# Idle products and turns among gate products, a longer fill at a branch, a later weight split: three reorderings in a two-layer trunk kernel

## The chip, the cores and the metric

The kernel runs on one core of a Trainium2 chip. The metric is the device time of one execution in microseconds. The core's engines are named as in the profile: PE is TensorE (its matrix products; PEld its weight loads), DVE is VectorE, ACT is ScalarE, POOL is GpSimd and SP is SyncE. Each has a queue of instructions of its own, which it works through in order.

## The reference

16 learned meta tokens are put ahead of a sequence of 512 tokens with 1024 features. Two layers follow, each with an RMSNorm, a combined input projection, a mixing branch, a SiLU gate and an output projection that is added to the stream; then a final norm.

```python
def gla_branch(xn, w_in, w_gate_up, b_gate, gnorm, w_out):      # 4 heads
    proj = xn @ w_in
    q, k, v, z, g_lr = jnp.split(proj, ...)                     # g_lr has 16 columns
    lg = jax.nn.log_sigmoid((g_lr @ w_gate_up + b_gate)) / GLA_TAU
    ...                                                         # chunks of 64 with decay exp(cumsum(lg))
    y = jax.nn.silu(z) * o
    return y @ w_out

def diff_branch(xn, w_in, lam_vecs, gnorm, w_out, rel_table, lambda_init):   # 8 heads
    q, k, v, z = jnp.split(xn @ w_in, 4, axis=-1)
    ...
        p = jax.nn.softmax(s, axis=-1)                          # two score maps per head
        a = p[:, :, 0] - lam * p[:, :, 1]
        return jnp.einsum('bhqk,bhkv->bhqv', a, vh)
    ...
    y = jax.nn.silu(z) * head_rms(o) * gnorm * (1 - lambda_init)
    return y @ w_out

h = concatenate([meta, x])
for i in range(2):
    h = h + (gla_branch, diff_branch)[i](rmsnorm(h, g_norm[i]), ...)
return rmsnorm(h[16:], g_final)
```

## The kernel before, in words

**Number format.** Every factor of a product is held as two parts, a rounded one and the rest: `split` (L264 on ACT makes the first, L265 on DVE the second; names end in h and l, as in `wh`, `wl`, `a11h`, `a11l`, and `x`). A product takes three passes (h·h, h·l, l·h). The sequence of 528 is worked on in two halves of 264 columns, so most PE instructions are 128x128 weights by 264 columns.

**Products.** A `Unit` computes a projection of 256 columns with seven block products in place of eight, out of sums of token blocks (`token_sums`, L743 to L752: `X["t1"]` to `X["t4"]`) and sums of weight blocks (`want_unit`, L325). Its block products accumulate in banks named `bx`, `by` and `bv` (L386); after some of them `partial` (L407, ACT, high priority) copies the bank out as `u`, and the next block product goes on adding in the same bank, so PE waits there for `u`. `add` (L432 to L436, DVE) makes the outputs. The first head's q, k and v are plain products instead (`plain_unit`, L825).

**Weights.** `Weights` is a queue of weight loads. A load (SP, one or two transfers of 512 KB) fills a `raw` buffer, of which there are two; its parts (`a11`, `sum`, `pair` and so on) are split as soon as there is room for them.

**Order.** PE's order is the order in which the code is written. `W` (a `Weaver`) holds products that are due later, and `W.fill(us)` takes products worth so many microseconds out of that queue and puts them between two steps. ACT and DVE are also ordered by hand up to the gate products (the block `ordered`); after that a scheduler orders them by priority, and `urgent` gives a call a higher one.

**The gate stage.** After the normalised tokens are turned (`turned`, L666) and split, the gate's 16 columns are computed for all tokens: eight steps k, each of two halves in two banks (`pgs`, L939), with `W.fill(0.6)` from the fourth step on, which takes v's products (L825). The banks are then read by ACT (L946, L949) and DVE (L947, L948, L950). v's second half is accumulated in the same two banks afterwards. `wur` (L953 on ACT, L954 on DVE) is the split of the gate's second factor. `raw_turn` (L654) turns the raw tokens of blocks 0, 3 and 4 on PE, and `raw_copy` (L660 on ACT, L662 on DVE) copies them to `hT`.

**The steepness branch.** A flag `fl` (L996, L997) says whether the decays are so steep that another way of computing scores is needed. PE carries it to one partition (L1220), DVE turns it into an integer `fi` (L1221), all engines load it (L1223) and branch (L1224). With these inputs the branch is not taken.

**The second layer's scores and values.** For each block of 128 tokens: scores and softmax (L1575 to L1582), a turn of the probabilities (L1590, L1591; `aT` and `am` on ACT and DVE), values (L355, L1606), norm (`output`: L1610, L1611 and L1614 on ACT, L1613 on POOL) and `rows` (L1620 on PE, L1623 on DVE). They run between the block products of the units of the next head.

Of the kernel before, what the change touches and what calls it, by code (L numbers as in the profile page):

```python
# [20 lines left out]
P = 128  # L21
# [187 lines left out]
def trunk(ctx, tc, x, meta, g_norm, gla_w_in, gla_w_gate_up, gla_b_gate, gla_gnorm, gla_w_out,  # L209
# [30 lines left out]
    def pb_pair():  # L240
        turns[0] += 1
        return [pb_tile(tag) for tag in (("bx", "bx") if turns[0] % 2 else ("bv", "by"))]

    def ps_tile():
        return T(ps_pool, [P, 512], F32, "ps")
# [12 lines left out]
        return run  # L258


    def split(hi, lo, src, scale=None):

        if scale is None:
            act.activation(hi, src, AF.Copy)  # L264
            dve.tensor_tensor(lo, src, hi.bitcast(F32), op=ALU.subtract)  # L265
        else:
            act.activation(hi, src, AF.Copy, scale=scale)
            dve.scalar_tensor_tensor(lo, src, scale, hi.bitcast(F32), op0=ALU.mult, op1=ALU.subtract)
# [39 lines left out]

    def block_pair(src):
        wh, wl = w_pair([P, 2, 512])
        split(wh, wl, src)
        return [[t[:, i, :] for t in (wh, wl)] for i in range(2)]

    def want_unit(w, c0):
        def single(tag, b):
            def fn(raw):
                t = [T(wp, [P, 512], F32R, tag + part, bufs=1) for part in "hl"]
                split(*t, raw[:, b, :])  # L320
                return t
            return Part(tag, fn)

        def add(o, a, b):
            dve.tensor_tensor(o, a, b, op=ALU.add)  # L325
# [20 lines left out]
    def want_plain(w, c0):  # L346

        return ws.want((w, c0), [Part("pair", lambda raw: block_pair(raw[:, 0::3, :])),
                                 Part("pair", lambda raw: block_pair(raw[:, 1:3, :]))])

    def mm3(ps, a, b, first=True, last=True, **kw):
# [39 lines left out]
    class Unit:  # L391
# [12 lines left out]
        @urgent  # L404
        def partial(self):
            t = T(up[0], [P, HT], F32, "u", bufs=3)[:, :self.n]
            act.activation(t, self.bx[:, :self.n], AF.Copy, scale=self.sc)  # L407
            return t

        def first(self):  # L410
# [165 lines left out]
    dve.memset(mhalf, -0.5)  # L576
    warm = ps_tile()

    def warm_up(n):
        for _ in range(n):  # L580
            pe.matmul(warm[:, :P], ones, ones, start=True, stop=True)

    warm_up(10)

# [14 lines left out]
    glr_raw = T(gp, [P, KT, RANK], F32, "a0")  # L599
    sp.dma_start(glr_raw, g_w_in[:, 6144:6160].rearrange("(k p) c -> p k c", p=P))  # L600

    v_first = [want_plain(g_w_in, 2048 + c) for c in (0, 256)]
    ws.held = 1
    ws.fetch()
    wup = v2[1][:, 0, :]
# [43 lines left out]
    def raw_turn(b):  # L649
        n = BLK[b][1]  # L650
        raws[b] = [ps_tile().rearrange("p (k c) -> p k c", k=4) for _ in range(2)]
        for i, pt in enumerate(raws[b]):
            for k in range(4):
                pe.transpose(pt[:, k, :n], xt[b][:n, (4 * i + k) * P:(4 * i + k + 1) * P], ident[:n, :n])  # L654

# [72 lines left out]
    for k0 in range(0, KT, 2):  # L728
        if k0 + 2 < KT:
            scaled_pair(k0 + 2)  # L730
        i, ks = k0 // 4, slice(k0 % 4, k0 % 4 + 2)
        for n, o in enumerate((X[("b11", "b21")[i]], (b12, X["b22"])[i])):
            split(o[0][:, ks, :], o[1][:, ks, :], xg[i][:, ks, n * HT:(n + 1) * HT])
        if k0 in (0, 4):
            ws.make_one()
    ws.held = 0
    x1, x2 = xg[0][:, :, :HT], xg[0][:, :, HT:]
    x3, x4 = xg[1][:, :, :HT], xg[1][:, :, HT:]
# [194 lines left out]
    heads = [Head() for _ in range(G_HEADS)]  # L933
    q_gla_v(0, heads[0])
    pgs = pb_pair()
    for k in range(KT):
        for n in range(2):
            for i, x in enumerate((X["b11"], b12) if k < 4 else (X["b21"], X["b22"])):
                pe.matmul(pgs[i][:112, :HT], glr[:, k, :], x[n][:, k % 4, :],  # L939
                          start=k == 0 and n == 0, stop=k == KT - 1 and n == 1)  # L940
        if k >= 3:
            W.fill(0.6)
    gh = T(gp, [P, L], F32R, "a0")
    for i, pg in enumerate(pgs):
        cs = slice(i * HT, (i + 1) * HT)
# [10 lines left out]
    carry = T(gp, [P, L], F32, "c0")  # L956
    dve.memset(carry, 1.0)
    dve.memset(carry[:, NM::P], 0.0)
    for b in (0, 3, 4):
        raw_turn(b)  # L960
        raw_copy(b, 0, dve)
        raw_copy(b, 1, act)
# [255 lines left out]
    W.fill(2.4)  # L1218
    pf = ps_tile()
    pe.matmul(pf[0:1, 0:1], fl[:, 1:2], one1, start=True, stop=True)  # L1220
    dve.tensor_copy(fi, pf[0:1, 0:1])  # L1221
    W.fill(1.5)
    steep = nc.values_load(fi[0:1, 0:1], min_val=0, max_val=P)  # L1223
    with tc.If(steep > 0, label="steep"):  # L1224

# [244 lines left out]
    def turned_back2(s, m, vt, first=False):  # L1470
        if not first:

            urgent(dve.tensor_copy)(vt[:, HT:HT + 8], vt[:, 2 * HT:2 * HT + 8])

        @urgent
        def post():
            end = L if first else 272
            pt, pm = to_tokens(vt, RBLK if first else HBLK, vt[:, end - 32:end])
            cs = slice(m * P, (m + 1) * P)
            split3(s.vm[:, cs], pm, 32, short[:, NM + 1:NM + 2])  # L1480
            split(s.v[0][:, :, cs], s.v[1][:, :, cs], pt.rearrange("p (b c) -> p b c", b=4))

        def done(pt, one, m):
            landed(s.v[0][:, :, m * P:m * P + P], s.v[1][:, :, m * P:m * P + P], pt, one)

        def last(pm):
            split3(s.vm, pm, 32, short[:, NM + 1:NM + 2])

        if first or s is heads[-1]:
            W.defer(2.2 if first else 1.4, post)  # L1490
        else:
            if m:
                s.leave = turn_by_dma(T(ep, [P, 2, 536], F32, "planes", bufs=1),
                                      [(slice(3, 1, -1), 0), (slice(1, None, -1), 272)], 240, 3.0 if heads.index(s) % 2 else 11.0, done, last)
            s.leave(m, vt[:, :536])
# [347 lines left out]
```

## Time and profile before

| | |
|---|---|
| median of 3 runs | 990.0 us (989.08 to 992.66) |
| the profiled execution | 992.34 us |
| its span in the trace | 990.5 us |
| mean granted clock of PE | 0.994 |
| PE busy | 971.0 us, 98% |
| DVE busy | 778.7 us, 79% |
| ACT busy | 614.2 us, 62% |
| POOL busy | 53.2 us, 5% |
| transfers | 96.24 MB, mean 97 GB/s |

Times in the trace count from the start of the span. A row of the timeline gives the start, the length, the engine, the line and the operation, the tiles out and in, and how many instructions are taken together; in brackets stands the engine's idle time before it and what ended that. The instructions of a row overlap, since a PE pass lasts longer than the distance to the next. PEclk is the share of full clock that PE was granted.

### The profile page before, as it was taken

The numbers are of one execution on the slowest core, as the hardware profiler recorded it, in microseconds if no ns is written. First come the engines' busy times: TensorE is split into PE (matmuls) and PEld (weight loads), VectorE is DVE, ScalarE is ACT, GpSimd is POOL, SyncE is SP. The second block draws the span as 40 slices with busy tenths as digits, with TensorE's granted clock in tenths as the row PEclk, the third lists the DMA queues.
The fourth block names the chain that finished last, engine by engine and source line by source line (L and its number), as shares of the span: only waits on it lengthen the run. The fifth ranks groups of instructions, "written<-read, shape, count | busy, mean of one in ns | idle before, by whom it ended". The sixth has DMA issues, their size and how long they took to land. (4 is left out here: it accounts for less than half of the span.)

```text
span 990.5 us, 18146 instructions
## 1 busy us (share of the span) xinstructions
PE 971.0 (98%) x7043; PEld 915.6 (92%) x7043; DVE 778.7 (79%) x1586; ACT 614.2 (62%) x1304; POOL 53.2 (5%) x68
## 2 busy tenths in 40 slices
PE   8999999999999999999999999999999999998997
PEld 7999999999999999999999998898988989988896
DVE  7888886887778788556998885977958879676785
ACT  7675865465547656536657675576764667654583
POOL 1000000001000100000000001001110000000001
PEclk8999999999999999999999999999999999999999
DMA  8223323742373322222332624235253352631222
GB/s 194 76 52 87 89 68 111 144 109 54 108 160 86 86 66 78 72 85 86 96 86 77 154 63 137 74 97 137 83 146 85 97 135 72 159 86 54 86 65 85
DMA packets 150472, 96.24 MB, mean 97 GB/s; under 512 B 33117, under 2 KB 136829, under 8 KB 150384
## 3 DMA queue, kind: packets, MB, share of 16 engines
q1 hardware_dynamic: 147504, 89.61, 33.7%
q10 hardware_dynamic: 2880, 5.46, 1.6%
q8 instruction: 55, 0.90, 0.4%
q14 instruction: 33, 0.27, 0.1%
HBM read 83.64 MB, written 7.57 MB: 92 GB/s over the span
## 5 line engine op out<-in xcount | busy, mean ns | idle before, releaser
L265 DVE TENSOR_TENSOR wl<-raw,wh 128x1024 fp32r<-128x1024 f32 x99 | 120.7, 1220 | 26.5 <-ACT wh L264 19.6
L264 ACT ACTIVATE wh<-raw 128x1024 fp32r<-128x1024 f32 x99 | 104.1, 1053 | 53.3 <-PE by L918 27.5
L386 PE MATMUL bx<-x,wh 128*128 128x264 f32 (+1 forms) x640 | 95.6, 287 | 3.0 <-ACT u L407 2.8
L386 PE MATMUL bv<-x,wh 128*128 128x264 f32 (+1 forms) x656 | 97.2, 286 | 0.2 <-DVE t L432 0.2
L386 PEld LDWEIGHTS bx<-x,wh 128*128 128x128 f32 x640 | 84.9, 189 | 4.1 <-ACT u L407 3.3
L386 PEld LDWEIGHTS bv<-x,wh 128*128 128x128 f32 x656 | 86.3, 189 | 0.7 <-DVE t L432 0.4
L376 PE MATMUL bx<-x,wh 128*128 128x512 f32 (+1 forms) x256 | 62.5, 386 | 0.0
L265 DVE TENSOR_TENSOR wl<-sum,wh 128x1024 fp32r<-128x1024 f32 x41 | 50.1, 1221 | 14.9 <-ACT wh L264 12.9
L407 ACT ACTIVATE u<-bx 128x264 f32<-128x264 f32 (+1 forms) x120 | 45.4, 379 | 25.1 <-PE bx L386 23.2
L1613 POOL TENSOR_TENSOR st<-st,mhalf 128x1 f32<-128x1 f32 x32 | 33.0, 1032 | 467.1 <-ACT on L1611 415.5
L1577 ACT ACTIVATE p<-p,st 128x528 f32<-128x528 f32 (+3 forms) x64 | 36.4, 568 | 31.1 <-DVE st L1575 30.7
L386 PE MATMUL bv<-x,wl 128*128 128x264 f32 (+1 forms) x328 | 55.2, 285 | 0.0
L386 PE MATMUL bx<-x,wl 128*128 128x264 f32 (+1 forms) x320 | 54.0, 287 | 0.0
L376 PEld LDWEIGHTS bx<-x,wh 128*128 128x128 f32 x256 | 44.5, 188 | 8.0
L264 ACT ACTIVATE wh<-sum 128x1024 fp32r<-128x1024 f32 x41 | 43.3, 1055 | 12.1 <-PE bv L386 4.5
L264 ACT ACTIVATE a11h<-raw 128x512 fp32r<-128x512 f32 x41 | 25.8, 628 | 38.5 <-DMA raw<-in_diff_w_in_dram 22.0
L386 PE MATMUL by<-x,a12h 128*128 128x264 f32 (+1 forms) x320 | 46.7, 285 | 0.0
L386 PE MATMUL bx<-x,a11h 128*128 128x264 f32 (+1 forms) x320 | 46.2, 285 | 0.0
L386 PEld LDWEIGHTS bv<-x,wl 128*128 128x128 f32 x328 | 45.9, 188 | 0.0
L386 PEld LDWEIGHTS bx<-x,wl 128*128 128x128 f32 x320 | 45.4, 190 | 0.5 <-DVE wl L265 0.2
L386 PEld LDWEIGHTS bx<-x,a11h 128*128 128x128 f32 x320 | 42.2, 188 | 0.8
L386 PEld LDWEIGHTS by<-x,a12h 128*128 128x128 f32 x320 | 41.8, 188 | 0.1
(475 smaller groups left out, 2640.4 us busy)
## 6 DMA issues: line engine op xcount, KB each, us to landing
raw<-in_gla_w_in_dram SPq DMA_DIRECT2D x48, 512.0 KB, 4.2
raw<-in_diff_w_in_dram SPq DMA_DIRECT2D x42, 512.0 KB, 5.6
raw<-in_diff_w_in_dram SPq DMA_DIRECT2D x11, 1024.0 KB, 6.1
raw<-in_gla_w_out_dram SPq DMA_DIRECT2D x8, 1024.0 KB, 5.3
raw<-in_diff_w_out_dram SPq DMA_DIRECT2D x8, 1024.0 KB
vd<-planes ACTq DMA_DIRECT2D x12, 268.0 KB, 3.5
vd<-keep ACTq DMA_DIRECT2D x8, 264.0 KB, 2.3
T<-bdr SPq DMA_DIRECT2D x8, 264.0 KB, 3.4
```

Source lines behind the costliest of these rows:

```text
L264: act.activation(hi, src, AF.Copy)
L265: dve.tensor_tensor(lo, src, hi.bitcast(F32), op=ALU.subtract)
L376: pe.matmul(bank, a[:, k, :], b[k] if n0 is None else b[k][:, n0 + i * nn:n0 + (i + 1) * nn], start=n == 0 and ks[0] == 0, stop=n == len(t ...
L386: pe.matmul(bank[:, :x[q].shape[2]], w[p][:, k * P:(k + 1) * P], x[q][:, k, :], start=first and i == 0, stop=i == len(PASSES) - 1, skip_gr ...
L407: act.activation(t, self.bx[:, :self.n], AF.Copy, scale=self.sc)
L1577: act.activation(p[:, :nk], p[:, :nk], AF.Exp, scale=-1.0, bias=st[:, m:m + 1], accum_out=st[:, 2 + m:3 + m])
L1613: pool.tensor_tensor(ms, ms, mhalf[:, :1], op=ALU.pow)
```

## The change

It has three parts.

**In the gate stage**, eleven products of a tile of ones with itself (`warm_up`) are put among the four gate products of the first step, into a bank that nobody reads. The fills begin at the second step instead of the fourth. The turns of token blocks 3 and 4 move from behind the gate products to places among steps 1 to 4, and their copies to `hT` are all made by ACT; only block 0 is still turned afterwards. DVE's half of the first split of v's weights (`keep`) is issued one step of x splits later.

**At the branch**, the fill between the flag's product and its load grows from 1.5 to 3.2 us, and DVE's conversion of the flag gets a higher priority.

**In the last head of the second layer**, the split of the first block (`a11`) of its v unit is issued after the last partial sum that was copied out (`issue_after(W.moved.ins)`) instead of as early as it can be.

```diff
+    kept = []
+
+    def split(hi, lo, src, scale=None, keep=False):
-        if scale is None:
+        if keep:
+            act.activation(hi, src, AF.Copy)
+            kept.append(lambda: dve.tensor_tensor(lo, src, hi.bitcast(F32), op=ALU.subtract))
+        elif scale is None:
...
-    def want_unit(w, c0):
+    def want_unit(w, c0, calm=False):
         def single(tag, b):
             def fn(raw):
                 t = [T(wp, [P, 512], F32R, tag + part, bufs=1) for part in "hl"]
-                split(*t, raw[:, b, :])
+                with tc.issue_after(W.moved.ins) if calm and b == 0 else ExitStack():
+                    split(*t, raw[:, b, :])
                 return t
...
         def partial(self):
             t = T(up[0], [P, HT], F32, "u", bufs=3)[:, :self.n]
-            act.activation(t, self.bx[:, :self.n], AF.Copy, scale=self.sc)
+            W.moved = act.activation(t, self.bx[:, :self.n], AF.Copy, scale=self.sc)
             return t
...
-    v_first = [want_plain(g_w_in, 2048 + c) for c in (0, 256)]
+    v_first = [want_plain(g_w_in, 2048 + c, c == 0) for c in (0, 256)]
...
         if k0 in (0, 4):
             ws.make_one()
+        if k0 == 2:
+            kept.pop()()
...
     pgs = pb_pair()
+    idle = pb_tile("bv")
+    turns_of = {(2, 2): (3, 1), (2, 3): (4, 0), (4, 0): (4, 1)}
     for k in range(KT):
         for n in range(2):
             for i, x in enumerate((X["b11"], b12) if k < 4 else (X["b21"], X["b22"])):
+                if k == 0:
+                    warm_up((3, 3, 1, 4)[2 * n + i], idle)
+                if (k, 2 * n + i) in turns_of:
+                    b, half = turns_of[k, 2 * n + i]
+                    raw_turn(b, [half])
                 pe.matmul(pgs[i][:112, :HT], glr[:, k, :], x[n][:, k % 4, :],
                           start=k == 0 and n == 0, stop=k == KT - 1 and n == 1)
-        if k >= 3:
+        if k >= 1:
             W.fill(0.6)
+        if k == 1:
+            raw_turn(3, [0])
+        if k == 5:
+            for b in (3, 4):
+                for i in range(2):
+                    raw_copy(b, i, act)
...
-    for b in (0, 3, 4):
+    for b in (0,):
         raw_turn(b)
...
-    dve.tensor_copy(fi, pf[0:1, 0:1])
-    W.fill(1.5)
+    urgent(dve.tensor_copy)(fi, pf[0:1, 0:1])
+    W.fill(3.2)
...
-        return W.add(Unit(want_unit(d_w_in, 2 * DI + 256 * hd), X, 1.0, dst, lambda i: turned_back2(s, i, vts[i])), 9.2)
+        u = want_unit(d_w_in, 2 * DI + 256 * hd, hd == D_HEADS - 1)
+        return W.add(Unit(u, X, 1.0, dst, lambda i: turned_back2(s, i, vts[i])), 9.2)
```

The changed kernel has other line numbers: L265 becomes L270, L268 L273, L386 L392, L407 L413, L747 L757, L748 L758, L825 L835, L946 to L950 become L969 to L973, L954 becomes L977, L1220 and L1223 become L1243 and L1246, and L1610, L1614 become L1634, L1638.

DVE's queue behind the last x splits, before. The banks of the gate products are `bx_314` and `bx_315`; `y` and `x` are token sums and their splits:

```order
L265 TENSOR_TENSOR x_4_80<-y_35_258,x_4_80 128x1056
L947 CAST a_20_157<-bx_314 16x264
L948 CAST a_20_157<-bx_314 16x264
L954 TENSOR_TENSOR z_392<-v_13_120,z_392 32x1024
L950 TENSOR_TENSOR a_20_157<-bx_314,a_49_380 16x264
L947 CAST a_20_157<-bx_315 16x264
L948 CAST a_20_157<-bx_315 16x264
L662 COPY hT_90<-ps_398 128x4x16
L662 COPY hT_90<-ps_410 128x4x128
L950 TENSOR_TENSOR a_20_157<-bx_315,a_49_380 16x264
L662 COPY hT_90<-ps_422 128x4x128
L748 TENSOR_TENSOR y_42_292<-y_42_292,y_35_258 128x4x264
```

The same place in the changed kernel:

```order
L270 TENSOR_TENSOR x_4_80<-y_35_258,x_4_80 128x1056
L758 TENSOR_TENSOR y_42_291<-y_42_291,y_35_258 128x4x264
L970 CAST a_20_157<-bx_314 16x264
L971 CAST a_20_157<-bx_314 16x264
L670 COPY hT_90<-ps_446 128x4x16
L977 TENSOR_TENSOR z_440<-v_13_120,z_440 32x1024
L973 TENSOR_TENSOR a_20_157<-bx_314,a_54_428 16x264
L970 CAST a_20_157<-bx_315 16x264
L971 CAST a_20_157<-bx_315 16x264
L273 SCALAR_TENSOR_TENSOR x_5_81<-y_42_291,x_5_81 128x1056
L973 TENSOR_TENSOR a_20_157<-bx_315,a_54_428 16x264
L762 TENSOR_TENSOR y_42_291<-y_42_291 128x4x264
```

The token sum of L748 (now L758) and the split of the next one (L273) stand ahead of the last read of the second bank, and two of the copies to `hT` are gone from this queue.

PE's queue at the branch, before (`by_1078` is the bank of the next unit's first product):

```order
L825 MATMUL bx_988<-x_3_79,wh_893 128x264
L1220 MATMUL ps_1044<-ones,fl_1003 1x1
L825 MATMUL bx_987<-x_2_78,wh_893 128x264
...
L825 MATMUL bx_988<-x_3_79,wl_894 128x264
L386 MATMUL by_1078<-x_1_77,a11h_904 128x264 x3
L1223 TENSOR_LOAD fi_1007
```

The same place in the changed kernel:

```order
L835 MATMUL bx_1000<-x_3_79,wl_906 128x264
L1243 MATMUL ps_1068<-ones,fl_1027 1x1
L392 MATMUL by_1090<-x_1_77,a11h_916 128x264 x8
L392 MATMUL by_1090<-x_1_77,a11l_917 128x264 x4
L392 MATMUL bx_1113<-x_2_78,a12h_1077 128x264 x8
L392 MATMUL bx_1113<-x_2_78,a12l_1078 128x264 x4
L392 MATMUL by_1090<-x_5_81,wh_1073 128x264 x6
L1246 TENSOR_LOAD fi_1031
```

The flag's product stands behind the plain unit's last product instead of 12 ahead of it, and 30 products stand between it and the load instead of 15.

ACT's queue at the start of the last head's units, before (`raw_13837` is the last head's v weights, `raw_13710` an earlier load, `bx_13881` the bank of the running unit):

```order
L264 ACTIVATE a11h_14046<-raw_13837 128x512
L1610 ACTIVATE ps_13909<-st_13657 128x1
L1611 ACTIVATE on_13920,st_13657<-ps_13909 128x257
L1614 ACTIVATE on_13920<-ps_13909,st_13657 128x256
L264 ACTIVATE wh_13970<-raw_13710 128x1024
L407 ACTIVATE u_13937<-bx_13881 128x264
L264 ACTIVATE a12h_14117<-raw_13837 128x512
```

In the changed kernel the row of `a11h` is gone from ahead of `on`, and stands further down:

```order
L1638 ACTIVATE on_13932<-ps_13921,st_13669 128x256
L269 ACTIVATE wh_13982<-raw_13722 128x1024
L413 ACTIVATE u_13949<-bx_13893 128x264
L269 ACTIVATE a12h_14129<-raw_13849 128x512
L269 ACTIVATE aT_2534_13970<-ps_13964 128x256
L368 ACTIVATE am_13969<-ps_13965 32x128
L369 ACTIVATE am_13969<-ps_13965 32x128
L413 ACTIVATE u_13998<-bx_13893 128x264
L269 ACTIVATE a11h_14058<-raw_13849 128x512
```

Two partial sums and the norm's steps now come before the first block's split; its DVE half moves likewise, from ahead of the weight sums (L325) to behind `yt` (L1623).

More of the change, by code (lines that the diff above doesn't have):

```diff
@@ L258, in urgent @@
         return run
-    def split(hi, lo, src, scale=None):
-        if scale is None:
+    kept = []
[4 more added lines that the diff above has]
+        elif scale is None:
             act.activation(hi, src, AF.Copy)
@@ L305, in halves_of, with block_pair @@
         return [Part("pair", lambda raw, ca=ca: split_w(raw, ca)) for ca in (0, c)]
-    def block_pair(src):
+    def block_pair(src, keep=False):
         wh, wl = w_pair([P, 2, 512])
-        split(wh, wl, src)
+        split(wh, wl, src, keep=keep)
         return [[t[:, i, :] for t in (wh, wl)] for i in range(2)]
-    def want_unit(w, c0):
+    def want_unit(w, c0, calm=False):
         def single(tag, b):
@@ L344, in want_unit, with want_plain @@
         return a11, a12, a22, s21, s43
-    def want_plain(w, c0):
-        return ws.want((w, c0), [Part("pair", lambda raw: block_pair(raw[:, 0::3, :])),
+    def want_plain(w, c0, keep=False):
+        return ws.want((w, c0), [Part("pair", lambda raw: block_pair(raw[:, 0::3, :], keep)),
                                  Part("pair", lambda raw: block_pair(raw[:, 1:3, :]))])
@@ L577, in trunk, with warm_up @@
     warm = ps_tile()
-    def warm_up(n):
+    def warm_up(n, t=None):
+        t = warm if t is None else t
         for _ in range(n):
-            pe.matmul(warm[:, :P], ones, ones, start=True, stop=True)
+            pe.matmul(t[:, :P], ones, ones, start=True, stop=True)
     warm_up(10)
@@ L647, in scaled, with raw_turn @@
             dve.tensor_scalar(o, xt[b][:n, i * 512:(i + 1) * 512], sums0[:n, 5 + b:6 + b], None, op0=ALU.mult)
-    def raw_turn(b):
+    def raw_turn(b, halves=range(2)):
         n = BLK[b][1]
-        raws[b] = [ps_tile().rearrange("p (k c) -> p k c", k=4) for _ in range(2)]
-        for i, pt in enumerate(raws[b]):
+        for i in halves:
+            pt = ps_tile().rearrange("p (k c) -> p k c", k=4)
+            raws.setdefault(b, []).append(pt)
             for k in range(4):
```

## The prediction

> **What bounds the kernel now.** I read the page's busy shares first, then the list of what TensorE (PE) waited for, then windows, then the timeline around each wait.
>
> ```profile
> PE 971.0 (98%) x7043; PEld 915.6 (92%) x7043; DVE 778.7 (79%) x1586; ACT 614.2 (62%) x1304; POOL 53.2 (5%) x68
> ...
> PE bx L386 <- ACT u L407: 2.8, 1, 2.8
> PE by L386 <- PEq L1224: 1.7, 1, 1.7
> ...
> PE bx L825 <- DVE a L950: 0.5, 1, 0.5
> ```
>
> PE is busy for 98% of the span. Only time in which PE stands still, or runs at half clock, can be won. The change aims at the two longest single waits (2.8 and 1.7 us), and at the gate stage, where PE seems busy. There the windows must be read with their clock (columns: window, length, busy us and instructions of PE, PEld, DVE, ACT, POOL, then PEclk, DMA share, GB/s):
>
> ```profile
> 12.29:15.70 3.41, 3.04 (x26) 2.61 (x25) 2.61 (x6) 2.82 (x7) 0.60 (x3) 1.00 1.17 290
> 15.70:19.12 3.42, 2.46 (x10) 1.50 (x10) 3.26 (x5) 3.42 (x7) 0.22 (x1) 0.99 1.10 210
> 19.12:22.53 3.41, 2.86 (x12) 2.40 (x12) 3.41 (x6) 3.36 (x6) 0.00 (x0) 0.50 0.39 21
> 22.53:25.95 3.42, 3.42 (x17) 3.42 (x17) 3.38 (x5) 0.14 (x1) 0.00 (x0) 0.51 0.56 90
> 80.54:83.95 3.41, 1.75 (x15) 1.57 (x14) 3.41 (x7) 0.77 (x2) 0.00 (x0) 1.00 0.05 12
> 906.57:909.98 3.41, 0.63 (x5) 0.64 (x6) 3.15 (x5) 2.70 (x8) 0.55 (x1) 1.00 0.02 6
> 909.98:913.40 3.42, 3.42 (x18) 3.42 (x18) 2.94 (x8) 0.90 (x4) 0.00 (x0) 0.50 0.00 0
> 913.40:916.80 3.40, 3.40 (x28) 3.36 (x28) 1.99 (x5) 1.75 (x6) 0.99 (x1) 1.00 0.00 0
> ```
>
> The bounds are multiples of 3.41 us from 19.12, where the clock steps. A window with 10 passes (15.70) or 5 (906.57) is followed by one at 0.50; one with 15 (80.54) is not; 12 passes at half clock leave it at half, 17 bring it back. So the clock follows how much PE did in the window before. A full window at half clock does 18 passes instead of 28, and costs at most 3.41 / 2 = 1.7 us.
>
> **A, the gate stage.** Before, PE ends the gate products, the transposes and the first half of v's products, and then stands until VectorE (DVE) has freed the second accumulator bank:
>
> ```profile
> 15.74 1.36 DVE L265 TENSOR_TENSOR x<-y,x 128x528 fp32r<-128x528 f32 x2 [0.42 <-ACT x L264]
> 17.22 1.23 DVE L265 TENSOR_TENSOR wl<-raw,wh 128x1024 fp32r<-128x1024 f32 x1
> ...
> 24.53 1.25 DVE L743 TENSOR_TENSOR y<-y 128x1056 f32<-128x1056 f32 x1
> ...
> 31.24 1.22 DVE L954 TENSOR_TENSOR z<-v,z 32x1024 fp32r<-32x1024 f32 x1 [1.46 <-ACT z L953]
> 32.49 0.42 DVE L950 TENSOR_TENSOR a<-bx,a 16x264 fp32r<-16x264 f32 x1
> ...
> 35.89 1.26 DVE L748 TENSOR_TENSOR y<-y,y 128x1056 f32<-128x1056 f32 x1
> 38.38 1.25 DVE L268 SCALAR_TENSOR_TENSOR x<-y,x 128x1056 fp32r<-128x1056 f32 x1
> 17.65 1.18 ACT L264 ACTIVATE x<-y 128x528 fp32r<-128x528 f32 x2
> 28.90 0.43 DVE L947 CAST a<-bx 16x264 fp32r<-16x264 f32 x1 [0.66 <-ACT a L946]
> 12.10 0.83 PE L581 MATMUL ps<-ones 128*128 128x128 f32 x6
> 13.71 1.91 PE L666 MATMUL ps<-ident,y 128*128 128x128 f32 x16
> 29.83 1.53 PE L654 MATMUL ps<-ident,v 128*128 128x128 f32 x12
> 34.44 0.28 PE L825 MATMUL bx<-x,wh 128*128 128x264 f32 x1
> 35.19 2.09 PE L825 MATMUL bx<-x,wh 128*128 128x264 f32 x15 [0.47 <-DVE a L950]
> ```
>
> PE's side gets faster. A 264-wide product costs (2.09 - 0.28) / 15 = 0.12 us at full clock, an idle pass (0.83 - 0.27) / 5 = 0.11, a transpose (1.53 - 0.27) / 11 = 0.115. From the end of the sixteen L666 transposes (about 15.6) to the end of v's first half there are 80 products (9.6 us), 11 idle products of two passes (2.5), 16 transposes (1.8) and the eight small ones of block 0 (0.6): 14.5 us, so 30.1 if PE never waits; with some waits for x I take 30.6. Before it was 34.56. The window from 15.70 gets about 13 more passes, so the half clock from 19.12 goes.
>
> But who frees the banks? DVE is what is late next. The moved wl makes it wait for ScalarE's (ACT) second x half (done 18.83, row at 17.65): about 0.4 us lost, so L743 starts at 24.9. From there, by before's spacings, L747 26.2, x 27.3. L748, which was behind the bank at 35.89, now stands ahead of it: 28.5. Then the casts at 29.7 and 30.15 (PE's last gate product ends at about 28.6, no wait), the small hT copy 30.6, L954 30.85, the first L950 32.1, the two casts to 33.4, L268's split (ahead of the bank now, 1.17) to 34.7, the second L950 to 35.1. PE's second product of v's second half waits for that: 35.1 to 35.3 against 35.19. The hT copies that went to ACT, and DVE's 0.66 and 1.46 of idle time in these rows, pay for L748 and L268 and nothing more. Gain: 0.0. DVE comes out some 2 to 3 us ahead, which nobody needs: in the list of waits above, PE's next one is the branch's.
>
> And PE now stands from 30.6 to 35.2, but for a product or so: 4.5 us, longer than the 2.85 at 906.5 that cost a window at half clock, and than the 1.66 in the branch that cost none. Cost: nothing, if PE's side is slower than worked; 0.8 to 1.7 by most positions of the 3.41 us window; 2.25 with the windows as in this trace (32.77 to 36.18 with only 1.1 us of work in it: 0.55 lost; 36.18 to 39.59: 1.7). I take 1.7, the row at 909.98. A: -1.7 (0 to -2.3).
>
> **B, the steepness branch.**
>
> ```profile
> 78.56 0.15 DVE L997 TENSOR_SCALAR fl<-fl 128x1 f32<-128x1 f32 x1
> 79.15 0.19 PE L1220 MATMUL ps<-ones,fl 128*1 128x1 f32 x2
> ...
> 81.68 0.14 DVE L1221 CAST fi<-ps 1x1 int32<-1x1 f32 x1
> ...
> 80.83 0.53 PE L386 MATMUL by<-x,a11h 128*128 128x264 f32 x3
> 83.01 0.84 PE L386 MATMUL by<-x,a11h 128*128 128x264 f32 x5 [1.66 <-PEq L1224]
> ```
>
> fi comes 3.1 us after fl (DVE does a wl and an x split between them), and PE takes its next product 83.01 - 81.82 = 1.19 after fi. Now 30 products (3.65 us) stand between L1220 and the load of fi instead of 15, and L1220 and the last decay product each stand 12 products later. On DVE a sum and a ks add (about 1.0 together) come in ahead of the cast: fi is 3.5 after fl. If fl comes as long after the last decay product as now (6.9, for L1220's 7.3), PE resumes at 6.9 + 3.5 + 1.19 = 11.6, with its products done at 7.3 + 3.65 = 10.95: 0.6 of the wait stays. DVE arrives less loaded, so I take 0.2. The price of the fill is none: the 15 products are only done earlier. On DVE and ACT the load of fi now stands behind a11, sum, the z add and raw (2.4 us), so the kd of the first scores comes later; PE has 69 products (8 us) before it reads kd. Gain 1.5 (1.0 to 1.66).
>
> **C, the last head's first block.**
>
> ```profile
> 905.68 0.63 ACT L264 ACTIVATE a11h<-raw 128x512 fp32r<-128x512 f32 x1 [4.14 <-DMA raw<-in_diff_w_in_dram]
> 906.22 0.16 ACT L1610 ACTIVATE ps<-st 128x1 f32<-128x1 f32 x1
> ...
> 908.91 0.38 ACT L407 ACTIVATE u<-bx 128x264 f32<-128x264 f32 x1
> 907.26 0.69 DVE L325 TENSOR_TENSOR sum<-raw 128x512 f32<-128x512 f32 x1 [0.23 <-DMA raw<-in_diff_w_in_dram]
> ...
> 910.67 0.41 DVE L265 TENSOR_TENSOR aT<-ps,aT 128x256 fp32r<-128x256 f32 x1
> 902.96 0.28 PE L1606 MATMUL ps<-vm,am 96*128 96x256 f32 x1
> 909.35 1.63 PE L386 MATMUL bx<-x,wh 128*128 128x264 f32 x8 [2.85 <-ACT u L407]
> ...
> 913.76 0.88 PE L355 MATMUL ps<-v,aT 128*128 128x256 f32 x6
> 920.89 0.38 PE L355 MATMUL ps<-v,aT 128*128 128x256 f32 x1 [0.16 <-DVE aT L265]
> ```
>
> ACT sits 4.14 us on a weight block, with L1610 and the partial sum u behind it; L1610's input was there at 903.24. From L1610 to PE's product are 909.35 - 906.22 = 3.13 us, so without a11h PE goes on at 906.4, and at once, since its queue reaches that product at 906.5: 2.85 won, and the 1.7 of half clock from 909.98.
>
> What is late next is DVE's queue. Its sum waits for the same load (second half, 907.26), and aT stands five instructions behind: 910.67 + 0.41 = 911.1, unchanged. PE's third L355 needs it; with full clock PE is there at 909.6 and waits 1.5. That product began at 914.0 before: 2.9 won there, in place of 4.5. Then ACT: L1610 of the next scores follows an hT that comes out of the same DVE queue at about 913.2; 2.7 us more (906.22 to 908.91) to the end of its wh, which now stands ahead of the k splits, 1.3 for these (0.63 per 128x512, by a11h), and aT at about 917.5; DVE's part stands behind a wl (1.23) and two k splits (0.69 each) that wait for these, about 919.2. PE wants it at 917.8. The product that began at 920.89 begins at 919.2: gain 1.7. a11h itself is needed only by the unit behind. C: 1.7, from 1.6 to 2.9 (if DVE gets to aT first).
>
> **The sum.** 0.0 - 1.7 + 1.5 + 1.7 = 1.5 us gained. The profiled execution took 992.34 (span 990.5 and 1.84 around it), 2.34 above the median of the runs, 990.0. It becomes 990.8; I take the 1.5 off the median: 988.5.
>
> **The rivals.**
>
> *A pays in full.* If DVE reached the banks at PE's pace, its six operations on them (0.42 to 0.43 each) would follow the last gate product at 28.6 through ACT: 31.6 instead of 35.2, 3.6 won and no standing PE. With B and C 6.8: 983.2. For it: PE's side really is 4 us earlier. Against: the order of DVE's queue is fixed.
>
> *The bank as worked, but no clock loss*: 986.8. For it: 80.54, where 15 passes kept the clock; with PE slower by 0.5 the first window gets there.
>
> *C is empty*: DVE and the next load hold PE to the old time; 990.2. Against: the third L355 is released at 911.1 in any case.
>
> *The clock falls anyway, and A turns into a loss.* If transposes and idle products did not hold the clock, 19.12 to 25.95 would stay at half with more work in it (two more fills of six products, 16 transposes: 3.2 us at full clock). DVE's cast at 29.7 tolerates a last gate product that ends 0.8 late; every microsecond more moves both banks. Ending at 33.0 instead of 28.6, it moves them by 3.5; with the 1.7 behind it, 5.2 against 3.2 from B and C: 992.0, slower. The rows speak against it: 12.29 to 15.70 held six idle passes, no other ordinary product, and twenty L666 transposes, and the window behind it ran at 0.99, where five ordinary passes (906.57) did not do. The Trainium skill, "TensorE: Matmul & The Clock Gate", Part 4: PE-mode transpose, says that a transpose does not count as PE-busy in the same way and doesn't engage the full clock. By that rule this rival would be the likely one; this trace's 0.99 after a window of transposes disagrees, and the measurement decides.
>
> **How the numbers follow.** Half a per cent, 5 us, is about what a measurement of this kernel can tell from no change. Forecast (988.5) 0.49, no clock loss (986.8) 0.18, A in full (983.2) 0.17, C empty (990.2) 0.07, A a loss (992.0) 0.09. Faster than 985.05: A in full, and 0.01 for "no clock loss" with C at 2.9 and B at 1.66 (985.4) and PE a little quicker: 0.18. Slower than 994.95: the last rival where the last gate product ends another 3 us later, 0.04. Within: 0.78. The range leaves out the outer parts of the first and the last rival: 983.0 to 992.0.
>
> **What would show it.** A: windows from 15.70 to 25.95 at 1.00, v's first half ended by about 30.6, PE waiting some 4 us for L950's successor until 35.2, a window at 0.50 from about 36. A resume before 33 there proves me wrong. B: no wait over 0.7 at the branch. C: no wait for u; 1 to 1.6 for aT at 911, again about 1.3 at 919, clock 1.00.

## The result, and the profile after

The changed kernel takes 994.53 us (median of 20 runs, 992.92 to 995.14), the kernel before 991.04 in the runs beside it (20 runs, 988.27 to 994.83). The ratio is 1.0032, 95% interval 1.0022 to 1.0042: slower by 0.32%, inside the half per cent, but outside the predicted range, and with the wrong sign. The profiled execution took 995.14 (span 993.4), where before's took 992.34 (990.5).

PE's busy time on the page, and the longest entries of what it waited for:

```profile
PE 972.2 (98%) x7065; PEld 917.5 (92%) x7065; DVE 778.1 (78%) x1584; ACT 615.6 (62%) x1306; POOL 52.2 (5%) x68
...
PE bx L835 <- DVE a L973: 4.8, 2, 2.5
...
PE bx L392 <- DVE fi L257: 1.1, 1, 1.1
...
PE ps L992 <- DVE t L998: 0.9, 1, 0.9
PE bx L392 <- ACT u L413: 0.8, 2, 0.6
...
PE ps L361 <- DVE aT L270: 0.7, 1, 0.7
```

The two waits that the change aimed at, 2.8 for u and 1.7 in the branch, are gone. In their place stand 4.8 at the gate's banks, 1.1 in the branch and 0.7 for aT.

**The gate stage.** The windows from before's clock steps, then those on the changed kernel's own steps (of PE alone: busy, passes, clock, DMA):

```profile
12.29:15.70 3.41, 3.13 (x29) 2.94 (x28) 2.87 (x8) 2.87 (x7) 0.79 (x2) 1.00 1.16 300
15.70:19.12 3.42, 3.42 (x32) 3.42 (x31) 2.53 (x4) 3.42 (x7) 0.24 (x1) 1.00 1.05 219
19.12:22.53 3.41, 3.41 (x31) 3.41 (x30) 3.41 (x6) 3.28 (x6) 0.00 (x0) 1.00 0.47 23
...
31.25:34.66 3.41, 0.39 (x1) 1.00 0.00 0
34.66:38.07 3.41, 2.25 (x10) 0.50 0.02 5
38.07:41.49 3.42, 3.42 (x18) 0.50 0.00 0
41.49:44.90 3.41, 3.41 (x30) 1.00 0.00 0
```

And DVE's and PE's timelines:

```profile
28.89 1.25 DVE L758 TENSOR_TENSOR y<-y,y 128x1056 f32<-128x1056 f32 x1
30.17 0.43 DVE L970 CAST a<-bx 16x264 fp32r<-16x264 f32 x1
...
31.34 1.22 DVE L977 TENSOR_TENSOR z<-v,z 32x1024 fp32r<-32x1024 f32 x1
32.59 0.42 DVE L973 TENSOR_TENSOR a<-bx,a 16x264 fp32r<-16x264 f32 x1
...
33.96 1.26 DVE L273 SCALAR_TENSOR_TENSOR x<-y,x 128x1056 fp32r<-128x1056 f32 x1
35.25 0.42 DVE L973 TENSOR_TENSOR a<-bx,a 16x264 fp32r<-16x264 f32 x1
...
33.07 0.39 PE L835 MATMUL bx<-x,wh 128*128 128x264 f32 x1 [2.48 <-DVE a L973]
35.82 2.54 PE L835 MATMUL bx<-x,wh 128*128 128x264 f32 x10 [2.36 <-DVE a L973]
```

PE ran at full clock to 30.6 (33.07 - 2.48) and then stood for 4.84 us but for one product. It went on at 35.82, where before it went on at 35.19, and did so at half clock until 41.49: v's first half ends four us earlier (30.59 instead of 34.56) and wins nothing, and two windows at half clock are paid.

**The branch**, on DVE and PE:

```profile
83.98 0.15 DVE L1020 TENSOR_SCALAR fl<-fl 128x1 f32<-128x1 f32 x1
84.06 1.23 DVE L270 TENSOR_TENSOR wl<-sum,wh 128x1024 fp32r<-128x1024 f32 x1
85.20 1.25 DVE L270 TENSOR_TENSOR x<-y,x 128x1056 fp32r<-128x1056 f32 x1
86.37 0.69 DVE L331 TENSOR_TENSOR sum<-raw 128x512 f32<-128x512 f32 x1
86.97 0.43 DVE L812 SCALAR_TENSOR_TENSOR ks<-bx,kd 128x264 f32<-128x264 f32 x1
87.31 0.14 DVE L257 CAST fi<-ps 1x1 int32<-1x1 f32 x1
...
87.45 1.25 PE L392 MATMUL bx<-x,a12h 128*128 128x264 f32 x8 [1.13 <-DVE fi L257]
```

The list names fi, but these a12h products stand ahead of the load of fi in PE's queue. They write a bx bank, and the first of the two ks adds, at 86.97, which reads one, ends at 87.40, 0.05 before PE goes on; in gate_only and branch_only, below, the list names ks for the same wait. That add stands behind the wl, the x split and the sum.

**The last head**, on ACT and PE:

```profile
909.46 0.17 ACT L1634 ACTIVATE ps<-st 128x1 f32<-128x1 f32 x1 [1.75 <-PE ps L1630]
...
912.18 0.38 ACT L413 ACTIVATE u<-bx 128x264 f32<-128x264 f32 x1
...
914.66 0.62 ACT L269 ACTIVATE a11h<-raw 128x512 fp32r<-128x512 f32 x1
...
923.76 0.39 PE L361 MATMUL ps<-v,aT 128*128 128x256 f32 x1 [0.69 <-DVE aT L270]
```

The partial sum u no longer waits behind the load, and the clock there is 1.00.

Where the time went is read from the start of the same PE rows in both traces. The changed kernel is behind by 2.9 us where before's reads 38.10, by 3.6 at 80, 3.8 at 110, 4.4 at 115, 5.7 at 323 and 6.2 at 891; then by 2.2 at 912 and 2.9 at the end. So in these two executions the gate and what follows cost 6.2, and the last head gives back 3.3.

### The profile page after: what moved, and what is told of

Same layout as the page of the kernel before. It is cut to its first block, busy times and chain, and to the rows that moved or that the text cites. A ratio compares the mean times of both kernels' runs of the same rounds, so it can differ in the third digit from the quotient of the medians.

```text
span 993.4 us, 18187 instructions
## 1 busy us (share of the span) xinstructions
PE 972.2 (98%) x7065; PEld 917.5 (92%) x7065; DVE 778.1 (78%) x1584; ACT 615.6 (62%) x1306; POOL 52.2 (5%) x68
## 5 line engine op out<-in xcount | busy, mean ns | idle before, releaser
L270 DVE TENSOR_TENSOR wl<-raw,wh 128x1024 fp32r<-128x1024 f32 x98 | 119.5, 1221 | 30.6 <-ACT wh L269 21.6
L392 PE MATMUL bv<-x,wh 128*128 128x264 f32 (+1 forms) x656 | 97.4, 287 | 0.5 <-DVE t L438 0.5
L392 PE MATMUL bx<-x,wh 128*128 128x264 f32 (+1 forms) x640 | 95.3, 286 | 1.0 <-ACT u L413 0.8
L392 PEld LDWEIGHTS bv<-x,wh 128*128 128x128 f32 x656 | 86.3, 189 | 1.3 <-DVE t L438 0.9
L392 PEld LDWEIGHTS bx<-x,wh 128*128 128x128 f32 x640 | 84.6, 188 | 2.3 <-ACT u L413 1.5
L413 ACT ACTIVATE u<-bx 128x264 f32<-128x264 f32 (+1 forms) x120 | 45.3, 379 | 24.8 <-PE bx L392 22.3
L270 DVE TENSOR_TENSOR wl<-sum,wh 128x1024 fp32r<-128x1024 f32 x41 | 50.0, 1220 | 12.0 <-ACT wh L269 10.6
L392 PE MATMUL bv<-x,wl 128*128 128x264 f32 (+1 forms) x328 | 55.0, 285 | 0.0
L392 PE MATMUL bx<-x,wl 128*128 128x264 f32 (+1 forms) x320 | 53.8, 285 | 0.0
L392 PE MATMUL by<-x,a12h 128*128 128x264 f32 (+1 forms) x320 | 46.7, 286 | 0.2 <-DVE t L438 0.2
L392 PE MATMUL bx<-x,a11h 128*128 128x264 f32 (+1 forms) x320 | 46.2, 285 | 0.0
L392 PEld LDWEIGHTS bv<-x,wl 128*128 128x128 f32 x328 | 45.8, 188 | 0.0
L392 PEld LDWEIGHTS bx<-x,wl 128*128 128x128 f32 x320 | 45.0, 188 | 0.5 <-DVE wl L270 0.2
L392 PEld LDWEIGHTS bx<-x,a11h 128*128 128x128 f32 x320 | 42.3, 188 | 0.8
L331 DVE TENSOR_TENSOR sum<-raw 128x512 f32<-128x512 f32 x41 | 28.2, 688 | 18.2 <-DMA raw<-in_gla_w_in_dram 11.4
```

What stands on the lines that cost most here:

```text
L392: pe.matmul(bank[:, :x[q].shape[2]], w[p][:, k * P:(k + 1) * P], x[q][:, k, :], start=first and i == 0, stop=i == len(PASSES) - 1, skip_gr ...
L413: W.moved = act.activation(t, self.bx[:, :self.n], AF.Copy, scale=self.sc)
```

## The experiments

Three rivals for the loss: the gate's half clock, the gate's DVE order, and the branch. And one question on the gain: whether the last head's 3 us are there outside the traces. All were timed beside the kernel before (its median there in brackets; then the ratio to it, with its 95% interval).

**One part at a time.** The gate alone:

```diff
-    urgent(dve.tensor_copy)(fi, pf[0:1, 0:1])
-    W.fill(3.2)
+    dve.tensor_copy(fi, pf[0:1, 0:1])
+    W.fill(1.5)
-        u = want_unit(d_w_in, 2 * DI + 256 * hd, hd == D_HEADS - 1)
+        u = want_unit(d_w_in, 2 * DI + 256 * hd, False)
```

> Only the gate stage's part of the change is made. Theory (banks and clock): DVE frees the second bank of the gate products at about 35.5 us, PE stands some 4.8 us in two pieces and then runs one to two windows of 3.41 us at half clock; 3.0 to 3.5 us slower than before. Rival (the loss sits elsewhere, as in the small waits at 113 and 306 to 323 us that the changed kernel's trace has): within 1 us of before.

Measured: 1001.23 (989.64), ratio 1.0114 (1.0094 to 1.0133), far slower than theory or rival had it. PE waits 4.7 for the banks again, and in the branch more than twice what it did before:

```profile
89.91 0.63 PE L392 MATMUL bx<-x,a12h 128*128 128x264 f32 x3 [1.13 <-DVE ks L812]
94.89 1.44 PE L392 MATMUL bx<-x,a12h 128*128 128x264 f32 x5 [4.36 <-PEq L1247]
...
91.86:95.27 3.41, 0.38 (x2) 0.50 0.76 180
```

The 4.36 are not the flag's lateness: `fi` was converted at 90.11, 3.67 us after `fl`, and PE loaded it at 90.28. Its branch instruction (COMPARE_BRANCH, L1247) then took 3.85 us, where it took 0.40 in before's trace and 0.49 in the changed kernel's; what held it was not found. Two windows at half clock, from 91.86, come with it. So this run does not price A alone. Its trace also has 2.05 us of waiting for normalised tokens at 13.41, which no other kernel with A has at that length; the profiled execution (1003.36) lies 2.0 us or more above the other three (1000.82 to 1001.35), so these may not have it.

The branch alone, in the kernel before:

```diff
-    dve.tensor_copy(fi, pf[0:1, 0:1])
-    W.fill(1.5)
+    urgent(dve.tensor_copy)(fi, pf[0:1, 0:1])
+    W.fill(3.2)
```

> Only the branch's part is made. Theory (a bank takes the place of the flag): PE's first product on the weights a12 needs the bank that DVE's second-last ks product frees, and that stands behind a wl split, an x split and a weight sum; PE still waits about 1.1 us, and the time is within 0.7 us of before. Rival (the prediction's step B): 1.5 us faster.

Measured: 989.31 (989.64), 0.9996 (0.9978 to 1.0013). In the trace the wait of 1.66 becomes one of 0.35 for ks and one of 0.17 at the branch itself, and PE gains about 0.9 us there. The bank does take the flag's place, but its wait is 0.35 instead of the expected 1.1; the interval (2.2 us faster to 1.3 slower) holds the theory's time and the rival's.

The last head alone:

```diff
-    def want_unit(w, c0):
+    def want_unit(w, c0, calm=False):
...
-                split(*t, raw[:, b, :])
+                with tc.issue_after(W.moved.ins) if calm and b == 0 else ExitStack():
+                    split(*t, raw[:, b, :])
```

> Only the last head's part is made. Theory: the 2.85 us wait for the partial sum and the half-clock window behind it go (4.2 to 4.5 us), and DVE's aT, which stands behind the weight sums that wait for the load, gives some of it back. By the prediction's step C 1.7 us faster; by the changed kernel's trace 2.9. In this kernel PE reaches the place some 6 us earlier than in the changed one, and the load should land where it did before, so 1.7 to 2.9, nearer to 1.7.

Measured: 990.29 (989.64), 1.0008 (0.9992 to 1.0024). In its trace u no longer waits behind the load, PE waits 0.7 for aT, and the last head is 3.1 shorter; the timed runs have none of it (at most 0.8 us faster by the interval).

**The gate's two terms.** DVE's order: the token sums and splits from k = 3 on, the split of `wur` and the copy of block 0 go behind the last read of the second bank.

```diff
-        dve.tensor_tensor(gs[32:32 + RANK, cs], ...
+        W.freed = dve.tensor_tensor(gs[32:32 + RANK, cs], ...
...
-            token_sums(k - 1)
+            with tc.issue_after(W.freed.ins) if k >= 3 else ExitStack():
+                token_sums(k - 1)
```

> The changed kernel, with DVE's token sums from the third on, the split of the gate's second factor and the copy of block 0 issued after the last read of the second bank (ACT's half of that split after ACT's last read). Theory (banks and clock): the second bank is free at about 32 us instead of 35.7, PE stands 1.5 to 2 us instead of 4.8 and keeps its clock or loses one window; 4 to 7 us faster than the changed kernel, so 1 to 4 us faster than before. Rival (PE's own extra products and turns cost the time): as the changed kernel, 3 us slower than before.

Measured: 990.81 (989.64), 1.0011 (1.0000 to 1.0022).

```profile
32.66 2.82 PE L835 MATMUL bx<-x,wh 128*128 128x264 f32 x15 [1.49 <-DVE a L973]
...
33.66:37.07 3.41, 3.41 (x18) 0.50 0.03 7
```

PE goes on at 32.66 instead of 35.82, with one window at half clock instead of two. Two thirds of the loss go (from 1.0032 to 1.0011), less than the 4 to 7 us expected: DVE's order, with the clock that follows from it, carries most of it.

The clock alone: 20 idle products between the halves of v's products, while PE stands anyway.

```diff
+            if i and rest:
+                warm_up(rest, ps_tile())
...
-                gens.append(W.add(plain_unit(u, evac)))
+                gens.append(W.add(plain_unit(u, evac, 0 if h else 20)))
```

> The changed kernel with 20 more idle products (40 passes, 4.5 us by the changed kernel's trace) where PE stands, between the first and the second half of v's first unit. Theory (half of the gate stage's loss is the clock): PE's second product of v's second half still starts at about 35.8 us, but the windows from 34.8 to 41.7 run at full clock; 2.3 to 2.9 us faster than the changed kernel. Rival (the clock in that stretch does not follow PE's idleness, or costs nothing): the same as the changed kernel, or later by what the idle products overrun.

Measured: 992.80 (990.59), 1.0022 (1.0005 to 1.0039). The bank is free nearly as late (PE goes on at 35.48 instead of 35.82), but the clock holds:

```profile
34.00:38.00 4.00, 3.36 (x29) 1.00 0.00 0
38.00:42.00 4.00, 4.00 (x36) 1.00 0.00 0
...
PE ps L994 <- DVE t L1000: 1.9, 1, 1.9
```

Where before's trace reads 40.83, PE is 0.2 behind before instead of 3.2. Of these 2.9 us 0.3 are the earlier bank, so the half clock cost some 2.6 in the trace. PE then meets a 1.9 us wait for DVE's t ahead of L994, with one window at half clock behind it (from 66.72), and at 110 it is 3.2 behind, only 0.6 less than the changed kernel. In the timed runs the intervals of the two overlap (1.0005 to 1.0039 against 1.0022 to 1.0042), so they do not decide between theory and rival.

**Everything mended**, first with banks_first's order, six idle products and, shown here, the fill and the token sum held back as a whole until the flag is converted:

```diff
-    urgent(dve.tensor_copy)(fi, pf[0:1, 0:1])
-    W.fill(3.2)
+    W.flag = urgent(dve.tensor_copy)(fi, pf[0:1, 0:1])
+    with tc.issue_after(W.flag.ins):
+        W.fill(3.2)
...
-    token_sums(5)
+    with tc.issue_after(W.flag.ins):
+        token_sums(5)
```

> The changed kernel with the bank reads first as in banks_first, six idle products in the wait that is left, and at the branch the conversion of the flag and the two ks products ahead of the splits that the fill issues (the fill and the last token split are issued after the conversion). Theory (banks, clock, bank at the branch): the wait of 1.13 us at the branch and the half-clock window behind the gate stage go; 2 to 3 us faster than banks_first, so 1 to 2 us faster than before. Rival (the rest of the loss comes from the shifted weave in the first layer, waits at 113 and 246 to 323 us): at most 1 us faster than banks_first.

Measured: 992.94 (990.59), 1.0017 (1.0000 to 1.0035). The gate was mended (PE 2.7 ahead of before at 38.10), but the x split that now stood behind the flag was needed by the fill itself: PE waited 3.5 for it at 89.13 and lost two windows of clock.

Then with only the fill's weight sums held back, the token sum called right behind the flag, and 6 idle products:

```diff
-                add(t[:, 1, :], raw[:, 2, :], raw[:, 3, :])
+            with tc.issue_after(W.flag.ins) if W.flag else ExitStack():
+                add(t[:, 1, :], raw[:, 2, :], raw[:, 3, :])
...
+    with tc.issue_after(W.flag.ins):
+        urgent(token_sums)(5)
     W.fill(3.2)
```

> As banks_first, with six idle products in the wait that is left at the banks, and at the branch the weight sums and the last token split issued after the conversion of the flag (only a wl split stays ahead of the ks products there). Theory (banks, clock, bank at the branch): no wait over 0.5 us at the branch and no half-clock window from 36 us on; 2 to 3.5 us faster than banks_first, so 1 to 2.5 us faster than before. Rival (DVE's work is only put off and PE waits for it a few microseconds later, as for x in all_mended): no faster than banks_first.

Measured: 987.96 (990.28), 0.9977 (0.9963 to 0.9991); run again as best2_again, below, 987.52 (990.28), 0.9973 (0.9962 to 0.9984). No wait in the branch, 0.7 at the bank, full clock. It is faster than the kernel before in both, and so faster than the changed kernel. Its trace has a wait of 1.50 us for z at 96.36 that the changed kernel's has not; whether that is DVE's work put off, as the rival has it, is open.

**Is the last head's gain there outside the traces?** First the load made later in the kernel before, by issuing it twice, and made lighter, with a quarter of its columns:

```diff
+        for again in range(2 if w is d_w_in and c0 == 2 * DI + 256 * (D_HEADS - 1) else 1):
             for i in range(2):
```

> The kernel before, with the load of the last head's v weights made twice in a row, so that its blocks land some 3 us later. If executions that are not profiled have the same stall as the profiled one (2.85 us at the partial sum), every microsecond of it is added: 3 to 5 us slower than before. If the load lands earlier in them, so that nothing waits, part of the 3 us is swallowed: 0 to 2 us slower.

```diff
+        n = 32 if w is d_w_in and c0 == 2 * DI + 256 * (D_HEADS - 1) else P
+        if n < P:
+            pool.memset(t.rearrange("p j (k c) -> p (j k) c", k=4)[:, :, n:], 0.0)
```

> The kernel before, with a quarter of the columns of the last head's v weights loaded and the rest set to zero by GpSimd, so that the load lands early (the output of that head is not the reference's). If executions that are not profiled have the stall of the profiled one, 3 to 4.5 us faster than before. If they have not, within 1 us of before; the profile itself should lose the wait in both cases.

Measured: 991.40 (990.59), 1.0001 (0.9984 to 1.0017), and 990.41 (990.59), 0.9988 (0.9968 to 1.0008). Neither decides. In the first the scheduler itself put the split behind u, so that u did not wait for the load; in the second the first block still came 4.66 us after its issue and u waited 2.1.

Then the kernel before and the last head alone once more, side by side, to see whether their traces repeat:

> The kernel before, unchanged: a second profile and 10 more times. Theory (the stall at the last head belongs to the profiled execution): the profile shows the wait of 2 to 3 us for the partial sum again, and its time stands 1.3 to 2.5 us above the median of the kernel's other executions. Rival (the first profile was just a slow execution): the profile's time lies near the median, with the wait in it.

> head_only once more, beside the kernel before in the same session. Theory (the stall belongs to the profiled execution): the profile's time lies at or below the kernel's median, and the ratio to before is within 0.2% of 1. Rival (the first comparison was bad luck): 2 to 3 us faster, a ratio of 0.997 to 0.998.

Measured: 990.82, 0.9999 (0.9983 to 1.0014), and 990.10, 0.9999 (0.9984 to 1.0014), both beside 990.28. The times are equal. In the traces u waits 3.0 in the one and not in the other, where the last head is 2.1 us shorter than in before, since now PE waits for aT:

```profile
910.60 0.75 PE L356 MATMUL ps<-v,aT 128*128 128x256 f32 x4 [1.16 <-DVE aT L265]
```

The profiled execution of before_again took 994.83, 4.1 above the median of the other eleven (more than the theory's 1.3 to 2.5), that of head_again 989.92, 0.3 below the median of its others.

Last, the fastest kernel with and without the last head's part, side by side:

```diff
-        u = want_unit(d_w_in, 2 * DI + 256 * hd, hd == D_HEADS - 1)
+        u = want_unit(d_w_in, 2 * DI + 256 * hd, False)
```

> The fastest kernel so far with part C alone undone: the first block of the last head's v weights is split ahead of the partial sums again; PE's and POOL's orders are the same. Profiled, every theory expects the old wait for u (about 2.9 us near 905) and a window at half clock back, so a span some 2.5 to 3 us over that of best2_again. If the load's late landing is there in every execution, the median is 2.5 to 3 us above that of best2_again (about 990.8 beside 988.0). If it is there in full only under the profiler, the medians agree within 0.7 us, and the profiled execution lies 2 to 3 us above this kernel's median.

> The fastest kernel so far, unchanged, beside best2_stall. If its gain is real, the ratio is again about 0.9977 of before; profiled execution within 0.5 us of its median, whatever holds for the load.

Measured: 987.72 without it (12 runs, 987.17 to 989.61) and 987.52 with it (986.71 to 987.95): 0.2 us apart, and the ratios to before are 0.9972 and 0.9973. So part C is worth nothing that the timed runs can tell, here as in head_only and head_again. But the stall of 2.9 that every theory expected in this profile is not there either, and the profiled execution lies 0.5 below its kernel's median. Its rows say why, by SP's issue of the load, ACT's split, DVE's sum and PE's product, with before's issue first:

```profile
899.77 0.99 SPq L280 DMA_DIRECT2D raw<-in_diff_w_in_dram  x2
```

```profile
898.24 0.99 SPq L285 DMA_DIRECT2D raw<-in_diff_w_in_dram  x2
902.59 0.63 ACT L269 ACTIVATE a11h<-raw 128x512 fp32r<-128x512 f32 x1 [2.58 <-DMA raw<-in_diff_w_in_dram]
904.34 0.69 DVE L332 TENSOR_TENSOR sum<-raw 128x512 f32<-128x512 f32 x1 [0.40 <-DMA raw<-in_diff_w_in_dram]
906.25 1.25 PE L394 MATMUL bx<-x,wh 128*128 128x264 f32 x8 [1.28 <-ACT u L415]
...
904.50:907.91 3.41, 2.13 (x18) 1.00 0.00 0
907.91:911.33 3.42, 3.42 (x31) 1.00 0.02 5
```

Same order on ACT as in the kernel before, same load; but here the first block came 4.35 us after its issue, where the trace of before has 5.91 (905.68 - 899.77). The stall is 1.28 instead of 2.85 and too short to cost a window of clock. From 916.6 on PE is where best2_again is, which waited 0.65 for aT instead. A short stall here only takes the place of the wait for aT.

## Why the prediction was wrong

**The baseline.** 990.0 was the median of three runs; twenty gave 991.04. That is 1.0 of the 6.0 us between 988.5 and 994.53. Another 1.7 is part C, and 3.3 are A and B: forecast together at 0.2 lost, measured at 994.53 - 991.04 = 3.5, with C at nothing.

**A: right mechanism, loss too small.** PE's side came out as worked (v's first half ended at 30.59, forecast 30.6), DVE held the bank nearly as worked (35.82, forecast 35.1 to 35.3), and PE stood 4.84 us (4.5). The mis-sized term is the clock: 1.7 was taken, and two windows, 34.66 to 41.49, cost about 2.6 in the trace by keep_clock; even the text's own upper end (2.25) was short, since the standing time covered one window almost whole and left only 10 passes in the next. What the sum had no term for came behind that: 0.6 at the bank, 0.9 at L992 (for DVE's L998), 0.6 for u at 115, and 1.3 between 115 and 323. In that stretch a weight sum waits 1.70 for its load instead of 0.45; it waits 1.0 to 1.7 in seven of the eight traces with A (0.45 in keep_clock's) and 0.4 to 0.8 in those without A, and its cause was not found. Of these only the clock and DVE's order were tested in time: 1.0032 goes to 1.0022 by the one, within the intervals, and to 1.0011 by the other. The two traces have 6.2 for A and B together where the times have 3.5; against head_again's trace, which has C and before's gate, it is 993.4 - 988.1 = 5.3. What makes up the rest is open.

**The rival on transposes** was rightly held unlikely: the clock stayed at 1.00 until PE had stood. By the changed kernel's own steps the window from 10.76 to 14.18 held transposes and idle products alone (22 passes), and the next was at 1.00. The Trainium skill, "TensorE: Matmul & The Clock Gate", Part 4: PE-mode transpose, has it that transposes don't engage the full clock; this 1.00, and the 0.99 behind before's window of twenty transposes and six idle passes, disagree, and the measurement decides. The traces list the transposes as MATMUL and do not show the mode in which they ran.

**B: right wait, wrong successor.** The flag came as worked, 3.33 us after fl (forecast 3.5). The step that failed is the one from there to 11.6, and to a wait of 0.2: it followed the flag alone. The fill's second row of products needs a bank that DVE must read first, and that read stands behind the same wl, x split and sum as the cast: 1.13, and 0.3 more at the branch itself. So in the changed kernel B gives 0 instead of 1.5 against before. What it is worth on top of A is open: gate_only is 8 us slower than the changed kernel by the ratios (1.0114 against 1.0032), but 3.85 us of its trace are a branch instruction that began when the flag was loaded already.

**C: right in the trace, nothing in the time.** The changed kernel's trace gave 3.3 (head_only's 3.1, head_again's 2.1) instead of 1.7: of the waits for aT that were to eat 2.8 of the 4.5, 0.7 came, since DVE's sum, which waits for the load, started 6.0 us after the load's issue where before's trace has 7.5. What failed is the step "I take the 1.5 off the median". The text had noted that the profiled execution lay 2.34 above the median, and still took a wait from that execution as one of every run.

Three things speak for a stall that belongs to profiled executions of the kernel before. The times with and without C are equal (head_only, head_again). The profiled executions of before_again, branch_only and head_light, where u waits 2.1 to 3.0, lie 4.1, 2.6 and 2.2 us above the median of their kernel's other runs, and those of head_only, head_late and head_again, where it does not, 1.7, 1.4 and 0.3 below. And the mean clock tells of half-clock windows in runs without a profile: the traces with none have 0.998 or 0.999, those with one 0.996 or 0.997, those with three or four 0.991 to 0.994. The 116 runs of the kernel before beside the experiments have 0.9960 on average, the 22 unprofiled ones of head_only and head_again 0.9962; a window that C removes in every run would make 0.0017 (half of 3.41 in 990 us).

But the load's time goes with the kernel too. From issue to DVE's sum it took 7.5 to 7.6 us in before, before_again and branch_only, 6.2 and 7.2 in the two traces of the last head alone, and 6.0 to 6.2 in seven traces with A. best2_stall is one of these seven, so its short stall says little of the kernel before. What the load took in the unprofiled runs was not seen, so this is inferred, not shown run by run.

## What to carry over

Moving work earlier on the bound engine wins nothing while another engine's queue decides when a buffer comes free: first put that read ahead in its queue (banks_first, and best2, which makes the change pay), and only then fill the gap. When a wait is filled, look up the buffers that the fill itself writes and who must read them. And compare a profiled execution with the median before taking a stall's price from it: where it lies above, what one sees may be that execution's own.

## What the runs showed of the hardware

The clock's windows are a grid of 3.413 us that is fixed within an execution (909.72 - 18.86 in before_again is 261 of them) and stands elsewhere in the next. With the same gate stage, four traces (before_again, branch_only, head_only, head_again):

```profile
18.86:22.27 3.41, 2.92 (x10) 0.50 0.43 29
22.27:25.69 3.42, 3.42 (x18) 0.50 0.42 54
...
909.72:913.13 3.41, 2.45 (x11) 0.50 0.00 0
913.13:916.55 3.42, 3.42 (x18) 0.50 0.00 0
```

```profile
21.64:25.06 3.42, 3.42 (x18) 0.50 0.52 18
25.06:28.47 3.41, 3.41 (x29) 1.00 1.04 287
```

```profile
17.03:20.44 3.41, 2.10 (x9) 1.00 0.74 109
20.44:23.85 3.41, 3.41 (x16) 0.50 0.47 4
23.85:27.27 3.42, 3.42 (x30) 1.00 0.84 223
```

```profile
17.63:21.04 3.41, 2.16 (x12) 1.00 0.44 53
21.04:24.46 3.42, 3.42 (x18) 0.50 0.39 7
```

The first half-clock window starts at 18.86, 21.64, 20.44 and 21.04, and the same gate stage has two of them in before and before_again, one in the other three. Where before's trace reads 38.10, those three are 0.8 to 1.0 us ahead of it and before_again is level: that much hangs on where the grid stands. The Trainium skill, "TensorE: Matmul & The Clock Gate", Part 1: The HAM clock gate, says that the window runs freely and does not start anew with the kernel; these traces agree. It goes with the spread of the times: the 116 runs of the kernel before lie between 987.4 and 995.7 at mean clocks of 0.992 to 0.999, the 17 at 0.994 or less all above 991.7; the 12 of best2_again, which has no long wait, between 986.7 and 988.0 at 0.996 to 0.999.

A smaller load was quicker than before's (4.66 us for the first block with a quarter of the columns, against 5.91) but no quicker than a quick full one (4.35 in best2_stall).
